# Float32 weights, unsplit, for the 64-slot experts: pairs of 64-column products on the two halves of the array, and the 192-slot expert in turns with the last one

## Chip, cores and metric

The kernel runs on one core of a Trainium2 chip. The metric is the device time of one execution in microseconds (us); the state before is given as the median of three runs and one profiled execution.

## What is computed

Two transformer blocks run over one sequence of 256 positions by 1024 features in float32. The first block has two layers (a mixer, then a feed-forward part); the feed-forward part of its second layer is a mixture of 8 SwiGLU experts, each position using the two that its router scores highest. The second block follows. The change touches the mixture of experts alone. Cut from the reference:

```python
def swiglu(x, w1, w3, w2):
    return (jax.nn.silu(x @ w1) * (x @ w3)) @ w2

def moe_swiglu(x, router_w, w1, w3, w2):            # t: 256 x 1024
    logits = (t @ router_w).astype(jnp.float32)
    top_v, top_i = lax.top_k(logits, TOP_K)         # 2 of 8
    gates = jax.nn.softmax(top_v, axis=-1)
    combine = jnp.sum(jax.nn.one_hot(top_i, N_EXPERTS, dtype=jnp.float32) * gates[..., None], axis=1)
    out = jnp.zeros_like(t)
    for e in range(N_EXPERTS):                      # w1[e], w3[e]: 1024 x 3584, w2[e]: 3584 x 1024
        out = out + combine[:, e:e + 1].astype(t.dtype) * swiglu(t, w1[e], w3[e], w2[e])
```

## The kernel before

**Slots.** After routing, experts 1 to 7 are ranked by how many positions chose them. Expert 0 and ranks 2 and 3 get 128 slots each, rank 1 gets 192 (128 and 64 more), ranks 4 to 7 get 64 each; if the positions don't fit, a second pass (`tc.If`) runs, which did not happen here. A one-hot matrix `oh` of positions by slots gathers the positions of an expert (`gather`, products of line 1169) and spreads the results back (`scatter`, line 1218).

**Steps.** An expert's 3584 hidden features go in 7 chunks of 512. One chunk of one expert is a step: it needs three tiles of 128 partitions x 4096 float32 (2 MB each): w1 and w3 for the up-products, w2 for the down-products. So there are 56 steps and 168 loads (`load`, line 155, all on SP's queue). They go through six buffers, `raw`, three in each of two pools, which the program takes in turn: a load waits until the load six before it has been read out. The down-products of a step stand behind the up-products of the next step.

**Groups.** Steps come in five groups: expert 0 in turns with rank 4, rank 2 with rank 5, rank 1 alone (its 128 and its 64 slots use each weight twice), rank 3 with rank 6, rank 7 alone. The tiles of the gathered positions are named g609, g876, g1167, g1365 and g1658 in the trace.

**Products.** Every weight is split into two float32r parts by `split`: ScalarE casts the high part, `wH` (line 170), VectorE subtracts to get the low part, `wL` (line 172). One split covers 128 x 1024; a step has 12 (4 for each of three tiles), and there are four buffers of each part. A 128-slot step forms three products for each tile of weights, `mm3`: high by high, low by high, high by low (lines 176 to 178). A 64-slot step puts the high and the low part of its 64 positions side by side as 128 stationary columns and forms two products, `mm2` (lines 1234 and 1235); the two halves of the result, copied out of PSUM (lines 1316 and 1317), are added by a product with a constant (`fold`, line 1336), before the activation (1339, 1340) and another split into `hO`. All moving operands here are 128 x 512. A 128-slot step transposes its hidden features four times (line 182) and splits them into `hH` and `hL`.

**Order.** The source says which instruction uses what; the order on each engine is made by the framework's planner when the kernel is built, from its own estimate of times. So transposes and folds stand among the up- and down-products. SP's loads stand in source order: w1, w3 of a step, then w2 of the step before.

**Elsewhere.** The mixers and the second block have float32 products that aren't split: line 943 (attention scores) takes its 64 contraction rows by turns from the lower and the upper half of the partitions, and 256 moving columns; line 747 has 64 x 64 products whose operands lie in one half of the partitions and whose results go by turns to PSUM partitions 0 to 63 and 64 to 127; lines 492 and 1548 use the whole array.

Of the kernel before, what the change touches and what calls it, by code (L numbers as in the profile page):

```python
# [105 lines left out]
class K:  # L106
# [1035 lines left out]
    def gather(self, xnH, xnL, pl, parts, into=None):  # L1142

        V, A, T = self.V, self.A, self.T
        if into is None:
            self.n += 1
            into = [self.mp.tile([P, 2, S], F32R, tag="oh", name=f"oh{self.n}", bufs=2), *self.xT_tiles(f"g{self.n}")]
        oh, gH, gL = into  # L1150
        for t in range(2):
            for over, r, slot0 in parts:
                for o in ((P, P + 64) if over else (0,)):
                    last = V.tensor_scalar(oh[:, t, o:o + (64 if over else P)], self.c("iota")[:, 0:64 if over else P],
                                           float(slot0), pl[:, t, r:r + 1], op0=OP.add, op1=OP.is_equal)
        if parts[0] == (False, 0, 0):
            self.hold = [(self.V, last)] * HOLD0

        c0 = P if parts[0][0] else 0
        w = P * (not parts[0][0]) + 64 * parts[-1][0]  # L1160
        m = 4 if w <= P else 2
        for k in range(0, KT, m):
            ks = slice(k, k + m)
            for src, low in ((xnH, False), (xnL, True)):
                b = self.bank()
                v = b.rearrange("p (k s) -> p k s", k=m)[:, :, 0:w]
# [4 lines left out]
                if not low:  # L1171
                    A.copy(gH[:, ks, c0:c0 + w], v)
                else:
                    if c0 == 0:
                        V.tensor_copy(gL[:, ks, 0:P], v[:, :, 0:P])
                    if c0 + w > P:
                        V.tensor_copy(gH[:, ks, P + 64:S], v[:, :, w - 64:w])
        return into

    def scatter(self, oh, cmp_, slots, accs, xacc, scale=1.0):  # L1180
# [5 lines left out]
        ohT, gcs, ys = [], [], []  # L1186
        for r, sl in slots:
            self.n += 1
            b = self.bank()
# [4 lines left out]
            o = self.mp.tile([P, S], F32R, tag="ohT", name=f"ohT{self.n}", bufs=2)  # L1194
            V.tensor_copy(o, b[:, 0:S])
            ohT.append(o)
# [3 lines left out]
            gcs.append(gc)  # L1200
        yield
        for i, (gc, acc) in enumerate(zip(gcs, accs())):

            h = tile(D, "rscr" if i else "yH")
            h = [h[:, ns] for ns in half]
            l = [self.wk(512, "ff", 3).bitcast(F32R) for n in half] if i else [tile(D, "yL")]
            l = l if i else [l[0][:, ns] for ns in half]
            for n in range(2):
                A.activation(h[n], acc[n], AF.Copy, scale=gc[:, 0:1])
                V.scalar_tensor_tensor(l[n], acc[n], gc[:, 0:1], h[n].bitcast(F32), op0=OP.mult, op1=OP.subtract)  # L1210
            ys.append((h, l))
        yield
        for t in range(2):
            for n in range(2):
                b = self.bank()
                for i in range(len(slots)):
                    for j, y in enumerate(ys[i]):
                        T.matmul(b, lhsT=ohT[i][:, t * P:(t + 1) * P], rhs=y[n], start=i == 0 and j == 0,
                                 stop=i == len(slots) - 1 and j == 1)
                V.scalar_tensor_tensor(xacc[:, t, half[n]], xacc[:, t, half[n]], scale, b, op0=OP.mult, op1=OP.add)  # L1220

    def experts(self, groups, xnH, xnL, pl, cmp_, xacc, between=None):
# [7 lines left out]
        main, over = slice(0, P), slice(P, 2 * P)  # L1230
# [6 lines left out]
        def down(job, c, hs, rd):  # L1237
            rd = rd.rearrange("p (f d) -> p f d", d=D)
            if c == 0:
                for o in hs:  # L1240
                    state["acc"][o] = [self.bank("acc") for n in range(2)]
            for j in range(4):
                H, L = self.split(rd[:, j:j + 1], (1, D))
                for n in range(2):
                    ns = slice(n * 512, n * 512 + 512)
                    ends = (c == 0 and j == 0, c == 6 and j == 3)
                    for o, h in hs.items():
                        acc = state["acc"][o][n]
                        if o:
                            mm2(acc, h[:, j], H[:, 0, ns], L[:, 0, ns], *ends)  # L1250
                        else:
                            self.mm3(acc, h[0][:, j], h[1][:, j], H[:, 0, ns], L[:, 0, ns], *ends)
# [3 lines left out]
        first = {id(g): (g[2][0], g[2][-1]) for g in groups}  # L1256
        pend, rest, into = None, None, None

        def gather(g, only=None):
            nonlocal into  # L1260
            parts = sorted(p for w, ps in g[0] for p in ps) if only is None else only
            into = self.gather(xnH, xnL, pl, parts, into if only and only[0][0] else None)

        late = None
        for n, (g, j, c) in enumerate(steps):
            w, parts = g[0][j]
            if between and g is groups[1]:
                between()
                between = None
            if (j, c) == first[id(g)][0]:  # L1270
                if len(g) > 3:

                    gather(g, g[3])
                    late = [p for p in sorted(p for w_, ps in g[0] for p in ps) if p not in g[3]]
                elif n == 0:
                    gather(g)
                oh, gH, gL = into
            if late and late[0] in parts:
                gather(g, late)
                late = None  # L1280
            raws = [self.load(w(c, i)) for i in range(2)]
            put = None
            if pend:
                (g0, j0, c0), hs = pend
                rd = self.load(g0[0][j0][0](c0, 2))
                if (j0, c0) == first[id(g0)][1]:
                    slots = [(r, over if o else main) for o, r, s in sorted(p for w_, ps in g0[0] for p in ps)]
                    put = self.scatter(state["oh"], cmp_, slots, lambda: [state["acc"][o] for o in sorted(state["acc"])],
                                       xacc, g0[1])
                    next(put)  # L1290
            banks, others = [], []
            kinds = [o for o, r, s in parts]
            for i in range(2):
                if False in kinds:
                    banks.append(self.bank())
                if True in kinds:
                    others.append(self.bank())
                x = raws[i].rearrange("p (k f) -> p k f", k=KT)
                for k in range(KT):
                    if k % 2 == 0:  # L1300
                        H, L = self.split(x[:, k:k + 2], (2, 512))
                    ends = (k == 0, k == KT - 1)
                    if banks:
                        self.mm3(banks[i], gH[:, k, main], gL[:, k, main], H[:, k % 2], L[:, k % 2], *ends)
                    if others:
                        mm2(others[i], gH[:, k, over], H[:, k % 2], L[:, k % 2], *ends)
# [3 lines left out]
            if banks:  # L1310
                s = self.wk(512, "ff", 3)
                A.activation(s, banks[0], AF.Silu)
                V.tensor_tensor(s, s, banks[1], OP.mult)
            if others:
                so = [self.wk(512, "ff", 3) for i in range(2)]
                A.copy(so[0], others[0])
                V.tensor_copy(so[1], others[1])  # L1317
            if n + 1 < len(steps) and steps[n + 1][0] is not g and len(steps[n + 1][0]) < 4:
                gather(steps[n + 1][0])
            if pend:  # L1320
                down(j0, c0, hs, rd)
            hs = {}
            self.n += 1
            if banks:
# [6 lines left out]
                hs[False] = (hH, hL)  # L1331
            if others:
                b = self.bank()
                for i in range(2):
                    for f in range(4):
                        T.matmul(b[:, i * 256 + f * 64:i * 256 + f * 64 + 64], lhsT=so[i][:, f * P:(f + 1) * P],  # L1336
                                 rhs=self.c("fold"), start=True, stop=True)
                s = self.wk(512, "ff", 3)[:, 0:256]
                A.activation(s, b[:, 0:256], AF.Silu)
                V.tensor_tensor(s, s, b[:, 256:512], OP.mult)  # L1340
                hO = self.mp.tile([P, 4, P], F32R, tag="hO", name=f"hO{self.n}", bufs=1)
                self.split(s.rearrange("p (f s) -> p f s", f=4), None, hO[:, :, 0:64], hO[:, :, 64:P])
                hs[True] = hO
# [3 lines left out]
            if (j, c) == first[id(g)][0]:  # L1347
# [4 lines left out]
        slots = [(r, over if o else main) for o, r, s in sorted(p for w_, ps in g0[0] for p in ps)]  # L1352
        put = self.scatter(state["oh"], cmp_, slots, lambda: [state["acc"][o] for o in sorted(state["acc"])], xacc, g0[1])
        down(j0, c0, hs, rd)
        list(put)

    def moe(self, xn):
# [21 lines left out]
        def pair(n, o, scale, order=None, now=None):  # L1379

            order = order or [(j, c) for c in range(7) for j in range(2)]
# [419 lines left out]
```

## Time and profile before

| | |
|---|---|
| median of 3 runs | 2092.45 us (2091.4 to 2101.74) |
| profiled execution | 2096.6 us, its span 2094.8 us |
| TensorE products (PE) | 1910.6 us busy, 91% of the span |
| VectorE (DVE) | 1613.3 us, 77% |
| ScalarE (ACT) | 1194.7 us, 57% |
| DMA | 484.79 MB, mean 231 GB/s over the span |
| mean granted TensorE clock | 0.944 of full speed |

PE is TensorE's row of products and PEld its row of weight loads; an engine's busy share is a mean over stages with different limits. The profile's page also cuts the span into 40 equal slices and gives for each the busy tenths of every engine and of the DMA engines, and the GB/s moved.

### The profile page before, as it was taken

How to read it: one execution, taken by the hardware profiler on the slowest of the kernel's cores; microseconds unless marked ns; L12 is line 12 of the kernel's file. 1: busy time of each engine (PE TensorE's matmuls, PEld its weight loads, DVE VectorE, ACT ScalarE, POOL GpSimd, SP SyncE). 2: the span in 40 equal slices, each digit the busy share in tenths (PEclk: the TensorE clock that was granted, in tenths of full speed). 3: DMA queues.
4: the chain of work that ended last, by engine and by line, in shares of the span. 5: the costliest groups of instructions: out<-in, count | busy, mean ns of one | idle time of the engine just before them, and what ended most of it. 6: DMA issues, size and time to landing. Idle time of an engine off the chain costs nothing. (4 is left out here: it accounts for less than half of the span.)

```text
span 2094.8 us, 28337 instructions
## 1 busy us (share of the span) xinstructions
PE 1910.6 (91%) x11072; PEld 1573.6 (75%) x11072; DVE 1613.3 (77%) x2131; ACT 1194.7 (57%) x1539; POOL 201.6 (10%) x128
## 2 busy tenths in 40 slices
PE   7878999977789999999999999999999886899998
PEld 6767899976577876776767888877677565779997
DVE  7895644579848998898888655699889887757776
ACT  3333444432335887777777554578777764645554
POOL 4241100043421000000000000000000003210000
PEclk9788999997788999999999999999999997889999
DMA  5321353542117999989998655589999953225451
GB/s 230 122 81 53 150 214 148 183 157 108 51 58 278 356 400 373 359 342 370 361 368 319 241 202 205 202 324 408 377 364 342 358 222 138 81 91 201 143 220 61
DMA packets 37581, 484.79 MB, mean 231 GB/s; under 512 B 4544, under 2 KB 5184, under 8 KB 8000
## 3 DMA queue, kind: packets, MB, share of 16 engines
q1 hardware_dynamic: 34992, 475.74, 59.8%
q10 hardware_dynamic: 2448, 7.17, 1.0%
q8 instruction: 89, 1.46, 0.3%
q14 instruction: 52, 0.43, 0.1%
HBM read 481.84 MB, written 1.05 MB: 231 GB/s over the span
## 5 line engine op out<-in xcount | busy, mean ns | idle before, releaser
L172 DVE TENSOR_TENSOR wL<-raw,wH 128x1024 fp32r<-128x1024 f32 x846 | 1001.3, 1223 | 257.4 <-ACT wH L170 253.2
L170 ACT CAST wH<-raw 128x1024 fp32r<-128x1024 f32 x896 | 917.3, 1049 | 489.6 <-PE mm L177 151.3
L177 PE MATMUL acc<-wL,hH 128*128 128x512 f32 x408 | 163.7, 402 | 0.2 <-DVE wL L172 0.2
L178 PE MATMUL acc<-wH,hL 128*128 128x512 f32 x408 | 160.8, 395 | 0.0
L176 PE MATMUL acc<-wH,hH 128*128 128x512 f32 x408 | 157.0, 398 | 0.7 <-ACT hH L170 0.7
L172 POOL TENSOR_TENSOR wL<-raw,wH 128x1024 fp32r<-128x1024 f32 x50 | 124.3, 2496 | 140.4 <-ACT wH L170 123.4
L188 POOL TENSOR_TENSOR sm_brs<-sm_brs,half_neg 128x1 f32<-128x1 f32 x8 | 12.1, 1517 | 1298.6 <-DVE sm_brs L186 1298.6
L176 PE MATMUL mm<-b2yH,wH 128*128 128x256 f32 x384 | 109.2, 285 | 0.0
L177 PE MATMUL mm<-b2yL,wH 128*128 128x256 f32 x384 | 109.1, 284 | 0.0
L178 PE MATMUL mm<-b2yH,wL 128*128 128x256 f32 x384 | 108.9, 284 | 0.0
L1235 PE MATMUL acc<-wL,hO 128*128 128x512 f32 x280 | 104.9, 418 | 0.8
L1234 PE MATMUL acc<-wH,hO 128*128 128x512 f32 x280 | 99.2, 398 | 1.4 <-DVE hO L172 1.4
L176 PE MATMUL mm<-y0H,wH 128*128 128x256 f32 x352 | 100.2, 285 | 0.0
L177 PE MATMUL mm<-y0L,wH 128*128 128x256 f32 x352 | 99.9, 284 | 0.0
L178 PE MATMUL mm<-y0H,wL 128*128 128x256 f32 x352 | 99.8, 284 | 0.0
L1336 PEld LDWEIGHTS mm<-cst,ff 128*128 128x128 f32 x560 | 75.2, 191 | 29.5 <-DVE ff L1317 19.5
L177 PEld LDWEIGHTS acc<-wL,hH 128*128 128x128 f32 x408 | 76.8, 188 | 17.4 <-DVE wL L172 1.1
L178 PEld LDWEIGHTS acc<-wH,hL 128*128 128x128 f32 x408 | 76.7, 188 | 17.4
L176 PEld LDWEIGHTS acc<-wH,hH 128*128 128x128 f32 x408 | 75.9, 188 | 17.8 <-ACT hH L170 1.4
L1336 PE MATMUL mm<-cst,ff 128*128 128x64 f32 x560 | 75.4, 269 | 13.8 <-DVE ff L1317 12.5
L176 PEld LDWEIGHTS mm<-b2yH,wH 128*128 128x128 f32 x384 | 74.1, 193 | 0.7 <-ACT b2yH L204 0.2
L177 PEld LDWEIGHTS mm<-b2yL,wH 128*128 128x128 f32 x384 | 74.1, 193 | 0.7 <-DVE b2yL L205 0.3
(569 smaller groups left out, 4294.4 us busy)
## 6 DMA issues: line engine op xcount, KB each, us to landing
raw<-in_moe_dram SPq DMA_DIRECT2D x168, 2048.0 KB, 9.6
raw<-in_ffn_dram SPq DMA_DIRECT2D x33, 2048.0 KB, 7.7
raw<-in_w_in_dram SPq DMA_DIRECT2D x13, 2048.0 KB, 8.1
raw<-in_w_o_dram SPq DMA_DIRECT2D x4, 2048.0 KB, 7.7
row<-in_ln_dram ACTq DMA_DIRECT2D x8, 512.0 KB, 3.7
raw<-in_w_out_dram SPq DMA_DIRECT2D x2, 2048.0 KB, 8.3
raw<-in_w_in_dram SPq DMA_DIRECT2D x3, 1024.0 KB, 4.9
raw<-in_ffn_dram SPq DMA_DIRECT2D x3, 1024.0 KB, 5.0
```

Of the source, the lines that this page charges most:

```text
L170: self.A.copy(H, src)
L172: (eng or self.V).tensor_tensor(L, src, H.bitcast(F32), OP.subtract)
L176: self.T.matmul(out, lhsT=lh, rhs=rh, start=start, stop=False)
L177: self.T.matmul(out, lhsT=lh, rhs=rl, start=False, stop=False)
L178: return self.T.matmul(out, lhsT=ll, rhs=rh, start=False, stop=stop)
L188: return self.G.tensor_tensor(out, out, self.half_neg.to_broadcast([P, n]), OP.pow)
L1234: T.matmul(out, lhsT=lh, rhs=rh, start=start, stop=False)
L1235: T.matmul(out, lhsT=lh, rhs=rl, start=False, stop=stop)
L1336: T.matmul(b[:, i * 256 + f * 64:i * 256 + f * 64 + 64], lhsT=so[i][:, f * P:(f + 1) * P], rhs=self.c("fold"), start=True, stop=True)
```

## The change

The 64-slot steps no longer use float32r parts. Their positions are gathered into one float32 tile `gx` (the low part is added to the copied high part), and the loaded weights go into the product as they are, float32, by `side`: two products for each tile of weights, each with the 64 positions as 64 stationary columns and one half of the weights' columns as the moving operand, the first writing PSUM partitions 0 to 63, the second 64 to 127. So a result of 64 x 512 lies in one PSUM tile of 128 x 256, and the activation, its product and two transposes work on 128 x 256. Splits, the two copies and the folds of these steps are gone; in the down-products the same is done with 1024 columns in two halves of 512, and one PSUM bank holds what two held. `scatter` reads the halves back by partition rows.

Rank 1 and rank 7 now form one group, in turns; the rank-1 steps use both forms (its 128 slots by `mm3`, its other 64 by `side`). So there are four groups, and their order is 0 and 4, 2 and 5, 1 and 7, 3 and 6.

```diff
     gather:
+            x = self.xp.tile([P, KT, 2, 64], F32, tag="xTL", name=f"gx{self.n}", bufs=1)
...
+                for i, r, slot0 in parts:
+                    u = v[:, :, at[i] - c0:at[i] - c0 + (64 if i else P)]
+                    d = i and gx[:, ks, i - 1]
+                    if i == 0:
+                        V.tensor_copy(gL[:, ks], u) if low else A.copy(gH[:, ks], u)
+                    elif low:
+                        V.tensor_tensor(d, d, u, OP.add)
+                    else:
+                        A.copy(d, u)
     experts:
-        def mm2(out, lh, rh, rl, start, stop):
-            T.matmul(out, lhsT=lh, rhs=rh, start=start, stop=False)
-            T.matmul(out, lhsT=lh, rhs=rl, start=False, stop=stop)
+        def side(out, lhsT, rhs, start, stop):
+            n = rhs.shape[1] // 2
+            for i in range(2):
+                T.matmul(out[i * 64:i * 64 + 64], lhsT=lhsT, rhs=rhs[:, i * n:i * n + n], start=start, stop=stop)
...
+            for i, h in hs.items():
+                acc = state["acc"][i]
+                for j in range(4):
+                    if i:
+                        side(acc[0], h[:, j % 2, (j // 2) * 64:(j // 2) * 64 + 64], rd[:, j], *ends)
+                    else:
+                        H, L = self.split(rd[:, j:j + 1], (1, D))
+                        for n in range(2):
+                            self.mm3(acc[n], h[0][:, j], h[1][:, j], H[:, 0, ns], L[:, 0, ns], *ends)
...
-                    if others:
-                        mm2(others[i], gH[:, k, over], H[:, k % 2], L[:, k % 2], *ends)
+                for p, b in nar:
+                    for k in range(KT):
+                        side(b[:, i * 256:i * 256 + 256], gx[:, k, p - 1], x[:, k], k == 0, k == KT - 1)
...
-                A.copy(so[0], others[0])
-                V.tensor_copy(so[1], others[1])
+            for p, b in nar:
+                sn.append(self.wk(512, "ff", 3)[:, 0:256])
+                A.activation(sn[-1], b[:, 0:256], AF.Silu)
+                V.tensor_tensor(sn[-1], sn[-1], b[:, 256:512], OP.mult)
...
-                        T.matmul(b[:, i * 256 + f * 64:i * 256 + f * 64 + 64], lhsT=so[i][:, f * P:(f + 1) * P],
-                                 rhs=self.c("fold"), start=True, stop=True)
...
+                    self.transpose(b[:, i * P:(i + 1) * P], s[:, i * P:(i + 1) * P])
+                h = self.mp.tile([P, 2, P], F32, tag="hN", name=f"hN{self.n}", bufs=1)
+                A.copy(h, b[:, 0:256].rearrange("p (f s) -> p f s", f=2))
     moe:
-                      ([(part(1), [(False, 1, 0), (True, 1, P)])], 1.0, chunks(0)),
-                      pair((3, 0), (6, 0), 1.0), ([(part(7), [(True, 7, 0)])], 1.0, chunks(0))], xnH, xnL, pl, cmp_, xn,
+                      ([(part(1), [(0, 1, 0), (1, 1, P)]), (part(7), [(2, 7, 0)])], 1.0, turns), (pair(3, 6), 1.0, turns)],
```

## Rows read from the trace of the kernel before

**Rows 1.** The page: busy us of each engine, then slices (busy tenths, GB/s).

```profile
PE 1910.6 (91%) x11072; PEld 1573.6 (75%) x11072; DVE 1613.3 (77%) x2131; ACT 1194.7 (57%) x1539; POOL 201.6 (10%) x128
...
DMA  5321353542117999989998655589999953225451
GB/s 230 122 81 53 150 214 148 183 157 108 51 58 278 356 400 373 359 342 370 361 368 319 241 202 205 202 324 408 377 364 342 358 222 138 81 91 201 143 220 61
```

**Rows 2.** Windows, the five groups: us, busy (x) by engine, PEclk, DMA share, GB/s.

```profile
657.00:892.00 235.00, 224.45 (x1034) 175.23 (x1034) 211.70 (x227) 183.03 (x206) 0.00 (x0) 0.99 0.96 371
892.00:1140.00 248.00, 234.41 (x1044) 176.66 (x1043) 222.16 (x235) 189.13 (x212) 0.00 (x0) 1.00 0.94 360
1140.00:1351.00 211.00, 210.39 (x1007) 175.20 (x1007) 128.35 (x147) 107.37 (x127) 0.00 (x0) 1.00 0.57 210
1351.00:1592.00 241.00, 233.05 (x1061) 181.19 (x1060) 217.54 (x222) 186.80 (x208) 0.00 (x0) 1.00 0.93 360
1592.00:1730.00 138.00, 120.14 (x502) 84.51 (x500) 119.12 (x132) 95.69 (x114) 0.00 (x0) 0.95 0.78 296
```

**Rows 3.** Groups by form, 892 to 1140: xcount | busy us, mean ns | idle before.

```profile
L172 DVE TENSOR_TENSOR wL<-raw,wH 128x1024 fp32r<-128x1024 f32 x170 | 197.2, 1218 | 4.7 <-ACT wH L170 4.5
...
L170 ACT CAST wH<-raw 128x1024 fp32r<-128x1024 f32 x168 | 171.5, 1050 | 25.9 <-PE mm L178 12.7 <-PE mm L1234 8.4 <-PE acc L178 2.9
...
L182 PE MATMUL mm<-cst,ff 128*128 128x128 f32 x28 | 4.2, 272 | 0.0
...
L1218 PE MATMUL mm<-yH,ohT 128*128 128x512 f32 x4 | 1.6, 393 | 0.0
```

**Rows 4.** Waits of SP's queue, 892 to 1140: us in total, times, longest.

```profile
SPq L155 <- DVE wL L172: 181.1, 35, 7.0
SPq L155 <- DVE ff L1340: 43.9, 7, 6.5
```

**Rows 5.** Timeline of PE in a 128-slot step: start us, us.

```profile
804.03 0.39 PE L176 MATMUL mm<-wH,g609H 128*128 128x512 f32 x1
804.26 0.40 PE L177 MATMUL mm<-wL,g609H 128*128 128x512 f32 x1
804.50 0.39 PE L178 MATMUL mm<-wH,g609L 128*128 128x512 f32 x1
804.73 0.39 PE L176 MATMUL mm<-wH,g609H 128*128 128x512 f32 x1
```

**Rows 6.** Lines with float32 operands: ns min/median/max; the first from the page.

```profile
L1336 PE MATMUL mm<-cst,ff 128*128 128x64 f32 x560 | 75.4, 269 | 13.8 <-DVE ff L1317 12.5
...
L1548 PE MATMUL acc<-xc,lw x32: 377/379/767, 1764.5 to 1789.5; 128*128 128x256 f32 x32
...
L492 PE MATMUL acc<-s,cst x16: 592/595/1219, 36.4 to 538.4; 128*128 128x512 f32 x16
```

**Rows 7.** Timeline of PE, three places with float32 products.

```profile
1764.54 0.59 PE L1548 MATMUL acc<-xc,lw 128*128 128x256 f32 x2
...
141.06 0.39 PE L178 MATMUL mm<-wH,x0L 128*128 128x512 f32 x1
141.38 1.13 PE L943 MATMUL mm<-aT,aT 64*128 64x256 f32 x8
...
151.41 0.65 PE L747 MATMUL acc<-s,cq 64*64 64x64 f32 x14
```

**Rows 8.** Windows in which the DMA engines were full; columns as in rows 2.

```profile
1410.00:1480.00 70.00, 67.95 (x309) 53.08 (x310) 66.23 (x64) 58.59 (x65) 0.00 (x0) 1.00 0.99 405
1430.00:1440.00 10.00, 10.00 (x47) 7.82 (x46) 9.60 (x10) 9.14 (x11) 0.00 (x0) 1.00 1.00 421
...
1620.00:1640.00 20.00, 18.46 (x78) 12.42 (x79) 18.30 (x19) 16.62 (x19) 0.00 (x0) 1.00 0.99 376
```

**Rows 9.** The last group: its up-products (line 1234), and a window.

```profile
L1234 PE MATMUL mm<-wH,g1658H x112: 387/394/628, 1592.7 to 1713.2; 128*128 128x512 f32 x112
...
1680.00:1700.00 20.00, 17.02 (x66) 12.68 (x65) 15.54 (x16) 13.04 (x15) 0.00 (x0) 0.83 0.90 349
```

More of the change, by code (lines that the diff above doesn't have):

```diff
@@ L1148, in gather @@
             self.n += 1
-            into = [self.mp.tile([P, 2, S], F32R, tag="oh", name=f"oh{self.n}", bufs=2), *self.xT_tiles(f"g{self.n}")]
-        oh, gH, gL = into
-        for t in range(2):
[L1152 to L1156, printed above, removed]
+            g = self.xp.tile([P, KT, S], F32R, tag="xTH", name=f"g{self.n}", bufs=1)
+            x = self.xp.tile([P, KT, 2, 64], F32, tag="xTL", name=f"gx{self.n}", bufs=1)
+            into = self.mp.tile([P, 2, 3 * P], F32R, tag="oh", name=f"oh{self.n}", bufs=2), g[:, :, 0:P], g[:, :, P:S], x
+        oh, gH, gL, gx = into
+        iota = self.c("iota")
+        for t in range(2):
+            for i, r, slot0 in parts:
+                for o, n in ((P, P),) if i == 0 else ((0, 64), (64, 64)) if i == 1 else ((2 * P, 64), (2 * P + 64, 64)):
+                    last = V.tensor_scalar(oh[:, t, o:o + n], iota[:, 0:n], float(slot0), pl[:, t, r:r + 1], op0=OP.add,
+                                           op1=OP.is_equal)
+        if parts[0] == (0, 0, 0):
             self.hold = [(self.V, last)] * HOLD0
-        c0 = P if parts[0][0] else 0
-        w = P * (not parts[0][0]) + 64 * parts[-1][0]
-        m = 4 if w <= P else 2
+        at = {0: P, 1: 64, 2: 2 * P}
+        c0 = min(at[i] for i, r, s in parts)
+        w = sum(64 if i else P for i, r, s in parts)
+        m = 512 // w if w != 192 else 2
         for k in range(0, KT, m):
@@ L1170, in gather @@
                                  start=t == 0, stop=t == 1)
[L1171 to L1177, printed above, removed]
+                for i, r, slot0 in parts:
+                    u = v[:, :, at[i] - c0:at[i] - c0 + (64 if i else P)]
[6 more added lines that the diff above has]
+                        A.copy(d, u)
         return into
@@ L1185, in scatter @@
         half = [slice(n * 512, n * 512 + 512) for n in range(2)]
-        ohT, gcs, ys = [], [], []
-        for r, sl in slots:
+        got = []
+        for i, r in slots:
             self.n += 1
+            sl = slice((P, 0, 2 * P)[i], (P, 0, 2 * P)[i] + P)
             b = self.bank()
@@ L1199, in scatter @@
             V.tensor_tensor(gc[:, 0:1], gc[:, 0:1], gc[:, 1:2], OP.add)
-            gcs.append(gc)
+            got.append((i, o, gc))
         yield
[L1202 to L1211, printed above, removed]
+        ys = []
+        for i, o, gc in got:
+            if i == 0:
+                h, l = tile(D, "yH"), tile(D, "yL")
+                h, l = ([x[:, ns] for ns in half] for x in (h, l))
+            elif i == 1:
+                h, l = ([x] for x in tile(D, "rscr").rearrange("p (a b) -> a p b", a=2))
+            else:
+                h, l = ([self.wk(512, "ff", 3).bitcast(F32R)] for n in half)
+            for n, acc in enumerate(accs()[i]):
+                A.activation(h[n], acc, AF.Copy, scale=gc[:, 0:1])
+                V.scalar_tensor_tensor(l[n], acc, gc[:, 0:1], h[n].bitcast(F32), op0=OP.mult, op1=OP.subtract)
+            ys.append((i, o, (h, l)))
         yield
@@ L1215, in scatter @@
                 b = self.bank()
[L1216 to L1219, printed above, removed]
+                ts = slice(t * P, (t + 1) * P)
+                rows = slice(n * 64, n * 64 + 64)
+                todo = [(o[:, ts], y[n]) if i == 0 else (o[rows, ts], y[0][rows]) for i, o, hl in ys for y in hl]
+                for j, (o, y) in enumerate(todo):
+                    T.matmul(b, lhsT=o, rhs=y, start=j == 0, stop=j == len(todo) - 1)
                 V.scalar_tensor_tensor(xacc[:, t, half[n]], xacc[:, t, half[n]], scale, b, op0=OP.mult, op1=OP.add)
@@ L1238, in down @@
+        def down(c, hs, rd):
             rd = rd.rearrange("p (f d) -> p f d", d=D)
             if c == 0:
[L1240 to L1245, printed above, removed]
-                    ends = (c == 0 and j == 0, c == 6 and j == 3)
[L1247 to L1252, printed above, removed]
@@ L1255, in experts @@
-        steps = [(g, j, c) for g in groups for j, c in g[2]]
[L1256 to L1264, printed above, removed]
+                for i in hs:
+                    state["acc"][i] = [self.bank("acc") for n in range(1 if i else 2)]
@@ new lines, in experts, with gather, put_of @@
+        steps = [(g, j, c) for g in groups for j, c in g[2]]
+        pend, rest, late, into = None, None, [], None
+        parts_of = lambda g: sorted(p for w, parts in g[0] for p in parts)
+        def gather(g):
+            nonlocal into, late
+            now = [p for p in parts_of(g) if len(g) < 4 or p in g[3]]
+            late = [p for p in parts_of(g) if p not in now]
+            into = self.gather(xnH, xnL, pl, now)
+        def put_of(g):
+            return self.scatter(state["oh"], cmp_, [p[0:2] for p in parts_of(g)], lambda: state["acc"], xacc, g[1])
@@ L1265, in experts @@
+        gather(groups[0])
         for n, (g, j, c) in enumerate(steps):
             w, parts = g[0][j]
+            new = n == 0 or steps[n - 1][0] is not g
             if between and g is groups[1]:
@@ L1269, in experts @@
                 between = None
[L1270 to L1277, printed above, removed]
+            if new:
+                oh, gH, gL, gx = into
             if late and late[0] in parts:
-                gather(g, late)
-                late = None
+                self.gather(xnH, xnL, pl, late, into)
+                late = []
             raws = [self.load(w(c, i)) for i in range(2)]
@@ L1285, in experts @@
                 rd = self.load(g0[0][j0][0](c0, 2))
[L1286 to L1289, printed above, removed]
+                if new:
+                    put = put_of(g0)
                     next(put)
-            banks, others = [], []
-            kinds = [o for o, r, s in parts]
+            main = [] if parts[0][0] else [self.bank() for i in range(2)]
+            nar = [(p, self.bank()) for p, r, s in parts if p]
             for i in range(2):
[L1294 to L1297, printed above, removed]
                 x = raws[i].rearrange("p (k f) -> p k f", k=KT)
-                for k in range(KT):
+                for k in range(KT if main else 0):
                     if k % 2 == 0:
                         H, L = self.split(x[:, k:k + 2], (2, 512))
-                    ends = (k == 0, k == KT - 1)
-                    if banks:
-                        self.mm3(banks[i], gH[:, k, main], gL[:, k, main], H[:, k % 2], L[:, k % 2], *ends)
-                    if others:
-                        mm2(others[i], gH[:, k, over], H[:, k % 2], L[:, k % 2], *ends)
+                    self.mm3(main[i], gH[:, k], gL[:, k], H[:, k % 2], L[:, k % 2], k == 0, k == KT - 1)
+                for p, b in nar:
+                    for k in range(KT):
+                        side(b[:, i * 256:i * 256 + 256], gx[:, k, p - 1], x[:, k], k == 0, k == KT - 1)
                 if i == 0 and rest:
@@ L1309, in experts @@
                     rest = None
-            if banks:
+            if main:
                 s = self.wk(512, "ff", 3)
[L1312 to L1315, printed above, removed]
-                A.copy(so[0], others[0])
-                V.tensor_copy(so[1], others[1])
-            if n + 1 < len(steps) and steps[n + 1][0] is not g and len(steps[n + 1][0]) < 4:
+                A.activation(s, main[0], AF.Silu)
+                V.tensor_tensor(s, s, main[1], OP.mult)
+            sn = []
+            for p, b in nar:
+                sn.append(self.wk(512, "ff", 3)[:, 0:256])
+                A.activation(sn[-1], b[:, 0:256], AF.Silu)
+                V.tensor_tensor(sn[-1], sn[-1], b[:, 256:512], OP.mult)
+            if n + 1 < len(steps) and steps[n + 1][0] is not g:
                 gather(steps[n + 1][0])
             if pend:
-                down(j0, c0, hs, rd)
+                down(c0, hs, rd)
             hs = {}
             self.n += 1
-            if banks:
+            if main:
                 b = self.bank()
@@ L1346, in experts @@
                 rest = put
-            if (j, c) == first[id(g)][0]:
+            if new:
                 state.update(acc={}, oh=oh)
@@ L1351, in experts @@
         rd = self.load(g0[0][j0][0](c0, 2))
-        slots = [(r, over if o else main) for o, r, s in sorted(p for w_, ps in g0[0] for p in ps)]
-        put = self.scatter(state["oh"], cmp_, slots, lambda: [state["acc"][o] for o in sorted(state["acc"])], xacc, g0[1])
-        down(j0, c0, hs, rd)
+        put = put_of(g0)
+        next(put)
+        down(c0, hs, rd)
         list(put)
@@ L1397, in moe @@
         with self.tc.If(most[0] > P):
-            self.experts([([(part(r), [(False, r, s)])], 1.0, chunks(0)) for r, s in (
+            self.experts([([(part(r), [(0, r, s)])], 1.0, alone) for r, s in (
                 (0, P), (1, WIDE), (2, P), (3, P), (4, 64), (5, 64), (6, 64), (7, 64))], xnH, xnL, pl, cmp_, xn)
```

35 lines of the change are left out of this document (13 added, 22 removed).

## The prediction, as it was put on record before the run

> **What bounds the kernel now.** I read the page first: PE is busy for 91% of the span, but the slices show where the others join it. In slices 13 to 22 the DMA engines are at eight to nine tenths and more, at 319 to 400 GB/s, and fall to five tenths for four slices [rows 1]. So I cut the experts by their tiles into the five groups [rows 2]. They last 1073 us of 2094.8, and they have three different limits.
>
> The three groups in turns take 235, 248 and 241 us for 14 steps each, 35 us for a pair of steps. In the second one DVE is busy 222 of 248 us, PE 234, DMA moves 360 GB/s [rows 2]. The groups by form say what DVE does: 170 low parts in 197.2 us, 1.16 us each, so 12 a step make 13.9 us and a pair 27.8 [rows 3]. ACT's casts wait for PE and SP's loads wait for the low parts: 181.1 us of SP's waits end with `wL`, another 43.9 with a vector instruction of the same steps [rows 4]. So DVE and PE hold each other up, and both hold the loads. The rank-1 group is bound by PE: 210.39 of 211 us, DVE at 128, DMA at 210 GB/s. The last group is the reverse: PE 120 of 138, the rest waiting for parts, hidden features and loads [rows 2].
>
> **The change, part by part.** *PE, a 128-slot step.* Its 72 products of 512 columns stay. Four starts lie 0.70 us apart for three intervals, 0.233 each [rows 5], so 16.8 us; four transposes at 4.2/28 = 0.15 us add 0.6 [rows 3]. Together 17.4.
>
> *PE, a 64-slot step.* Its 48 products of 512 columns (11.2 us) and the folds go. What comes is float32 on half the array, which no row shows in just this shape; I build it from two facts. First, the fold has 8 products in 35 steps, 280, and the trace has 560 records: a float32 product is two records. One lasts 377 ns for 256 columns and 592 for 512 [rows 6], so 215/256 = 0.84 ns a column, and two whole-array records of 256 columns begin 0.59 - 0.38 = 0.21 us apart [rows 7]. A product of 256 columns therefore takes 0.427 us, two of them 0.853 if they follow each other. Second, whether the halves run side by side. Eight records of line 943, in turns on the two halves of the rows, take 1.13 us, so (1.13 - 0.38)/7 = 0.107 us each, half of 0.21. For column halves line 747 is the nearest: 14 records of 64 columns in 0.65 us, (0.65 - 0.22)/13 = 0.033 each, where 64 x 0.84 = 0.053 would be one after the other [rows 7]. So the bounds for a pair of 256 columns are 0.427 (side by side) and 0.853 (in turn); I take 0.427, because both kinds of half show overlap. The weight loads of 64 columns are inside those 0.033 us. A step has 16 such pairs for up and 4 of twice the width for down, 24 units: 10.25 us, with two transposes 10.55. In turn it would be 20.8.
>
> *Switching.* Line 943 starts 0.32 us after the product before it, not 0.23 [rows 7], so going from the whole array to half costs 0.1; six switches in a pair of steps, 0.6 us. The Trainium skill says in "TensorEngine Tiling (Array Packing)", Key Properties, that changing the tiling mode drains TensorE; it speaks against this change, and if a switch cost a whole 0.39 us product, six would make 2.3. The row stands nearer to the small price, and the sum goes by the row.
>
> *A pair then.* PE: 17.4 + 10.55 + 0.6 = 28.6 us. DVE: 12 low parts instead of 24, 13.9 us and some 2 of small work; ACT likewise. Neither bounds any more. The loads of a 64-slot step now go free when PE has read them, not when DVE has: SP waits for PE. That is no delay by itself: at 5.27 us a load (below) a buffer may be held for four loads' time, 21 us, after it landed before the queue runs dry, and PE needs 3.4 us for each of w1 and w3. What can be late next is the split of the 128-slot w2: the first product needs a cast (1.05) and the second a low part (1.22) [rows 3], and where these stand behind the activation of the 64-slot step, PE idles up to 3 us a pair. From both sides: 0 and 3; I take 1.5, since ACT and DVE are half idle but queue in order. PE: 30.1.
>
> *DMA.* A pair loads 12.58 MB. At full DMA engines the windows show 405 GB/s over 70 us, 421 at best and 376 at worst [rows 8]: 31.1, 29.9 and 33.5 us. I take the middle of best and worst, 398: 31.6 us, or 5.27 a load. So a pair becomes DMA-bound, 31.6 against 35.
>
> *The groups.* 0 and 4: six loads are in before it starts, so PE sets 7 x 30.1 = 210. 2 and 5: 7 x 31.6 = 221. 3 and 6: 221. 1 and 7: PE does 17.4 + 2 x 10.55 + 0.9 = 39.4, with 1 us of stalls 40.4, times seven 283; in the pairs the gather and scatter at a border lie under DMA, here they are on PE, a scatter's 16 products (four rows like line 1218's 1.6) and a gather about as much, 7: 290. The end: 16.8 us from the last group's last up-product to 1730 [rows 2, 9]; the down-products no longer wait for splits there, but two sets of slots are scattered instead of one: 13. Gather's extra adds and copies, eight of each per group, lie on the freed ACT and DVE; on the path they would be 2 us a group.
>
> Sum: 210 + 221 + 290 + 221 + 13 = 955 against 1073, 118 us less. The profiled execution took 2096.6 us, 1.8 around its span and 0.2% above the median of 2092.45; 118 off it is 1978.6, and off the median **1974 us**.
>
> **The rivals.** *The halves run in turn (slower).* Place: every `side` pair. With 0.853 a 64-slot step costs 20.8, a pair 38.8, the rank-1 pair 59.9: 3 x 272 + 426 + 16 = 1258, 185 more: 2277. It decides at 15.5 us a step, 0.635 a unit: from there on the change is no gain. For it: line 747's operands span 64 partitions, here both moving streams come from all 128. Against it: [rows 7]. The change would not do what it says then; 1 in 10.
>
> *DMA gives no more than it gives now.* At 360 GB/s [rows 2] a pair takes 35.0: 215 + 245 + 300 + 245 + 17 = 1022, so 2041. For it: the DMA share is already 0.93 to 0.96 in those groups, and one full window has only 376. Against it: 405 for 70 us with the same kind of loads, while DVE was as busy as ever. The Trainium skill, "DMA: Bandwidth & Descriptors", Where 436 GB/s comes from, says that for HBM to SBUF the HBM side binds at about 358 GB/s per core; the 405 and 421 of this trace lie above that, so it can't be a ceiling for this core alone. 15 in 100.
>
> *PE waits for loads and loses its clock.* In the last group, where PE was 17.0 of 20 us busy with waits between, the granted clock was 0.83 for 20 us [rows 9], a mix of 1.2 and 2.4 GHz. At 0.83 the pair's PE work is 34.4 us: 3 x 241 + 290 + 14 = 1027, 2046. Against it: PE's share in a pair would be 28.6/31.6, higher than there, and a slower PE closes the gaps that slowed it. 8 in 100.
>
> **Chances and range.** My forecast has 67 in 100, its own range 1940 to 2010 (stalls 0 to 3, DMA 421 to 376). With the best DMA and no stalls it is 200 + 209 + 281 + 209 + 9 = 908, or 1927. The range goes from 1925 to 2050, taking in the slow DMA and the clock. The three runs spread over 0.5%, so 0.5% is about what a measurement tells from no change. Faster 0.88, within 0.5% 0.02 (a partly lost overlap near 0.635), slower 0.10.
>
> **What would show it.** In the changed kernel's trace: records of 128 x 256 and 128 x 512 on 128 rows and 64 columns, two for each product, two starts within some 0.22 us for 256 columns (right) or one (wrong); 336 fewer low parts of line 172's form; SP's loads waiting for PE rather than for `wL`; 390 GB/s or more through three groups and some 310 in the group of ranks 1 and 7; 31 to 32 us a pair, 39 to 41 in that group. It is wrong if a 64-slot step's PE time is far from 10.5, if GB/s stays near 360 with loads queued, or if the clock leaves 1.00 inside the groups.

## The result

The changed kernel takes 1997.78 us (median of 4 runs, 1994.05 to 2001.83), the kernel before 2092.05 on the same chip: ratio 0.9548, 95% interval 0.9509 to 0.9588, 94 us less. The forecast was 1974 in a range of 1925 to 2050, so the sign and the range held and the gain is 24 us smaller than forecast. The profiled execution took 2001.22 us, 95.4 less than the one before.

The page of the changed kernel (busy us of each engine; DMA busy tenths and GB/s in 40 slices; the lines of the new products, of the low parts, and of the silu of the 64-slot step):

```profile
PE 1819.5 (91%) x11670; PEld 1408.2 (70%) x11670; DVE 1197.6 (60%) x1717; ACT 842.3 (42%) x1176; POOL 203.4 (10%) x128
...
DMA  6320536352204799999999777787999944134551
GB/s 241 118 94 23 190 137 243 127 215 85 95 13 169 282 430 418 388 393 355 363 393 384 300 297 305 307 342 315 365 414 390 399 156 164 43 135 171 185 195 64
...
L172 DVE TENSOR_TENSOR wL<-raw,wH 128x1024 fp32r<-128x1024 f32 (+1 forms) x510 | 616.3, 1229 | 261.9 <-ACT wH L170 250.7
...
L1247 PE MATMUL mm<-raw,gx 128*64 128x256 f32 x2240 | 252.3, 381 | 0.0
...
L1247 PE MATMUL acc<-raw,hN 128*64 128x512 f32 x560 | 127.5, 597 | 0.0
L1321 ACT ACTIVATE ff<-mm 128x256 f32<-128x256 f32 x35 | 13.5, 385 | 247.8 <-PE mm L1247 247.8
```

VectorE is 416 us less busy than in [rows 1], ScalarE 352, PE only 91. The records are those that the prediction named: 35 x 64 and 35 x 16, two for a product. But one line was not expected: ScalarE stood idle for 247.8 us ahead of the 35 silu of line 1321.

The same windows as [rows 2], now four groups and the end (us, busy by engine, granted clock, DMA share, GB/s):

```profile
655.00:875.00 220.00, 208.33 (x1164) 147.00 (x1163) 117.23 (x133) 102.09 (x123) 0.00 (x0) 0.98 0.96 390
875.00:1112.00 237.00, 219.72 (x1165) 149.84 (x1163) 120.64 (x146) 100.86 (x126) 0.00 (x0) 0.96 0.95 374
1112.00:1399.00 287.00, 287.00 (x1744) 184.07 (x1743) 129.56 (x140) 108.05 (x139) 0.00 (x0) 1.00 0.79 309
1399.00:1614.00 215.00, 203.45 (x1105) 138.26 (x1104) 108.76 (x111) 91.86 (x106) 0.00 (x0) 0.98 0.97 388
1614.00:1632.00 18.00, 15.67 (x70) 8.75 (x66) 10.19 (x18) 6.61 (x9) 0.00 (x0) 1.00 0.02 7
```

They sum to 977 us against 1073: 96 less, the whole gain. Against the forecast: 220 for 210, 237 for 221, 287 for 290, 215 for 221, 18 for 13. The rank-1 group came out as worked out, with PE busy throughout. In the second group PE is busy for 93%, VectorE for half of the time; the DMA engines' share is 0.95, but they move only 374 GB/s, where slices of the same kernel show 430. What waits there is seen in the timeline of one pair of steps. ScalarE first (start us, us; in brackets the idle time before it and what ended that):

```profile
936.01 0.39 ACT L1321 ACTIVATE ff<-mm 128x256 f32<-128x256 f32 x1 [6.48 <-PE mm L1247]
937.37 0.37 ACT L1342 COPY hN<-mm 128x256 f32<-128x256 f32 x1 [0.98 <-PE mm L182]
...
953.41 0.59 ACT L1316 ACTIVATE ff<-mm 128x512 f32<-128x512 f32 x1
962.06 0.59 ACT L170 CAST hH<-mm 128x512 fp32r<-128x512 f32 x1 [8.06 <-PE mm L182]
969.13 0.39 ACT L1321 ACTIVATE ff<-mm 128x256 f32<-128x256 f32 x1 [6.48 <-PE mm L1247]
970.49 0.37 ACT L1342 COPY hN<-mm 128x256 f32<-128x256 f32 x1 [0.98 <-PE mm L182]
970.76 3.89 ACT L170 CAST wH<-raw 128x1024 fp32r<-128x1024 f32 x4
```

And PE in the same stretch:

```profile
961.95 7.13 PE L1247 MATMUL mm<-raw,gx 128*64 128x256 f32 x64
970.02 0.44 PE L182 MATMUL mm<-cst,ff 128*128 128x128 f32 x2 [0.94 <-DVE ff L1322]
971.86 1.22 PE L176 MATMUL acc<-wH,hH 128*128 128x512 f32 x2 [1.41 <-ACT wH L170]
973.12 0.80 PE L177 MATMUL acc<-wL,hH 128*128 128x512 f32 x1
```

A pair lasts 33.12 us here (936.01 to 969.13). At 962.65 ScalarE is done with the hidden features and idles for 6.48 us, until the up-products of the 64-slot step are finished; only behind silu and copy come the four casts of w2 of the 128-slot step, whose down-products PE is to do next. So PE waits 0.94 us for the silu's product and 1.41 for the first cast, and in this pair the granted clock falls right after: 0.57 over the 8 us from 971 to 979, where the down-products are. Summed over the group, PE's waits by cause are 8.5, 5.6 and 2.3 us, 16.4 in six pairs:

```profile
PE acc L176 <- ACT wH L170: 8.5, 6, 1.5
PE mm L182 <- DVE ff L1322: 5.6, 6, 0.9
PE acc L177 <- DVE wL L172: 2.3, 5, 0.5
```

### The profile page after: what moved, and what is told of

It reads as the page before. It is cut to its first block, busy times and chain, and to the rows that moved or that the text cites. A ratio compares the mean times of both kernels' runs of the same rounds, so it can differ in the third digit from the quotient of the medians.

```text
span 1999.4 us, 28155 instructions
## 1 busy us (share of the span) xinstructions
PE 1819.5 (91%) x11670; PEld 1408.2 (70%) x11670; DVE 1197.6 (60%) x1717; ACT 842.3 (42%) x1176; POOL 203.4 (10%) x128
## 5 line engine op out<-in xcount | busy, mean ns | idle before, releaser
L172 DVE TENSOR_TENSOR wL<-raw,wH 128x1024 fp32r<-128x1024 f32 (+1 forms) x510 | 616.3, 1229 | 261.9 <-ACT wH L170 250.7
L170 ACT CAST wH<-raw 128x1024 fp32r<-128x1024 f32 x560 | 577.5, 1051 | 401.7 <-PE mm L177 154.0
L1247 PE MATMUL mm<-raw,gx 128*64 128x256 f32 x2240 | 252.3, 381 | 0.0
L1247 PEld LDWEIGHTS mm<-raw,gx 128*64 128x64 f32 x2240 | 156.6, 137 | 85.6 <-issue 10.8
L176 PE MATMUL acc<-wH,hH 128*128 128x512 f32 x408 | 163.8, 416 | 19.8 <-ACT wH L170 19.0
L176 PE MATMUL mm<-wH,g 128*128 128x512 f32 x448 | 177.1, 395 | 0.0
L177 PE MATMUL mm<-wL,g 128*128 128x512 f32 x448 | 175.1, 391 | 0.0
L178 PE MATMUL mm<-wH,g 128*128 128x512 f32 x448 | 174.8, 390 | 0.0
L1247 PE MATMUL acc<-raw,hN 128*64 128x512 f32 x560 | 127.5, 597 | 0.0
L1321 ACT ACTIVATE ff<-mm 128x256 f32<-128x256 f32 x35 | 13.5, 385 | 247.8 <-PE mm L1247 247.8
L1322 DVE TENSOR_TENSOR ff<-ff,mm 128x256 f32<-128x256 f32 x35 | 14.7, 421 | 157.2 <-ACT ff L1321 157.2
```

Of the source, the lines that this page charges most:

```text
L170: self.A.copy(H, src)
L172: (eng or self.V).tensor_tensor(L, src, H.bitcast(F32), OP.subtract)
L176: self.T.matmul(out, lhsT=lh, rhs=rh, start=start, stop=False)
L177: self.T.matmul(out, lhsT=lh, rhs=rl, start=False, stop=False)
L178: return self.T.matmul(out, lhsT=ll, rhs=rh, start=False, stop=stop)
L1247: T.matmul(out[i * 64:i * 64 + 64], lhsT=lhsT, rhs=rhs[:, i * n:i * n + n], start=start, stop=stop)
```

## The experiments

**Theory A**: ScalarE's order sets the pair: w2's casts stand behind the silu of the 64-slot step, PE idles, and the clock that it loses makes the next products slower still; DMA is not the bound. **Rival B**, the forecast's own: a pair is bound by its six loads. **Rival C**: the halves overlap only in part. The changed kernel was run again on the chip of experiments 1 to 3; experiments 4 to 6 ran on another (before: 2085.53), so ratios are compared there.

> The changed kernel once more, as the base for the others of this call: 1994 to 2002 us, a pair of steps in the group of ranks 2 and 5 at 33 us, in the first two pairs of the last group 28.2.

1993.25 us, ratio 0.9528 (0.9495 to 0.9562).

**1. w2's casts ahead of the silu.** The down-products of the waiting 128-slot step are issued ahead of the 64-slot step's activation, and the silu is held behind their last cast:

```diff
-        self.A.copy(H, src)
+        self.cast = self.A.copy(H, src)
...
+            if pend and not main:
+                down(c0, hs, rd)
...
-                A.activation(sn[-1], b[:, 0:256], AF.Silu)
+                with self.tc.issue_after(self.cast.ins) if pend and not main else nullcontext():
+                    A.activation(sn[-1], b[:, 0:256], AF.Silu)
...
-            if pend:
+            if pend and main:
                 down(c0, hs, rd)
```

> In steps of 64 slots alone, the casts of the waiting 128-slot w2 are put ahead of the activation on ScalarE, nothing else. Theory A (ScalarE's order is what costs a pair 33 us where 28.2 is possible: w2 lies in its buffer 10 us and more while ScalarE waits for the 64-slot up-products): some 14 pairs lose 4 to 5 us each, 1928 to 1945 us, granted clock 1.00 through the groups, a pair at 28.2 to 29.5. Theory B (the loads set the pace, and the order only hides it): pairs stay at 31 or more, 1975 to 1995 us. If theory A holds the loads show 425 to 433 GB/s as the next limit.

1942.86 us (1940.78 to 1944.23), ratio 0.9269 (0.925 to 0.9289): 50 us less than the changed kernel, 153 less than the one before. ScalarE and PE in a pair of this kernel:

```profile
942.14 0.59 ACT L170 CAST hH<-mm 128x512 fp32r<-128x512 f32 x1 [8.07 <-PE mm L182]
942.62 3.89 ACT L170 CAST wH<-raw 128x1024 fp32r<-128x1024 f32 x4
949.20 0.39 ACT L1324 ACTIVATE ff<-mm 128x256 f32<-128x256 f32 x1 [2.70 <-PE mm L1247]
...
970.30 0.59 ACT L170 CAST hH<-mm 128x512 fp32r<-128x512 f32 x1 [8.07 <-PE mm L182]
```

```profile
942.03 7.13 PE L1247 MATMUL mm<-raw,gx 128*64 128x256 f32 x64
949.09 0.73 PE L176 MATMUL acc<-wH,hH 128*128 128x512 f32 x2
949.65 0.40 PE L177 MATMUL acc<-wL,hH 128*128 128x512 f32 x1
...
954.81 0.38 PE L182 MATMUL mm<-cst,ff 128*128 128x128 f32 x2
```

The four casts now run beside the 64 records, the down-products follow them without a gap, and a pair is 28.16 us (942.14 to 970.30). The edit moved more than ScalarE's casts: on PE, too, the 24 down-products now stand ahead of the two transposes of the 64-slot step (954.81), which before stood first and waited for the silu's product. No run parts the two orders. The windows of the five stretches, and of four pairs:

```profile
655.00:863.00 208.00, 204.14 (x1166) 145.80 (x1165) 117.47 (x137) 101.34 (x124) 0.00 (x0) 0.99 0.97 403
863.00:1077.00 214.00, 212.50 (x1174) 147.06 (x1175) 123.53 (x149) 101.92 (x129) 0.00 (x0) 0.99 1.00 422
1077.00:1362.00 285.00, 285.00 (x1732) 182.36 (x1731) 127.10 (x138) 106.14 (x137) 0.00 (x0) 1.00 0.80 317
1362.00:1562.00 200.00, 200.00 (x1113) 137.53 (x1113) 114.46 (x117) 95.57 (x111) 0.00 (x0) 1.00 0.97 403
1562.00:1577.00 15.00, 13.66 (x62) 7.89 (x61) 5.78 (x13) 2.33 (x4) 0.00 (x0) 0.99 0.47 196
...
926.00:1039.00 113.00, 113.00 (x635) 78.78 (x634) 64.92 (x61) 56.12 (x65) 0.00 (x0) 1.00 1.01 430
```

922 us in all, 55 less than after the change, 53 of them in the three groups that take 128 and 64 slots in turns and at the end. PE is busy for all of the last row at full clock, with DMA at 430 GB/s: the bytes are the same as in the changed kernel, so its 374 were no ceiling. A holds, for the order on ScalarE and PE together; B is refuted.

**2. One half after the other.** All products of a step's up-chain for one half of the array, then all for the other; the same products and bytes:

```diff
-        def side(out, lhsT, rhs, start, stop):
+        def side(out, lhsT, rhs, start, stop, half=None):
...
-            for i in range(2):
+            for i in range(2) if half is None else [half]:
...
-                    for k in range(KT):
-                        side(b[:, i * 256:i * 256 + 256], gx[:, k, p - 1], x[:, k], k == 0, k == KT - 1)
+                    for e in range(2):
+                        for k in range(KT):
+                            side(b[:, i * 256:i * 256 + 256], gx[:, k, p - 1], x[:, k], k == 0, k == KT - 1, e)
```

> Up-products of the 64-slot steps: all 8 products of one half of the array, then all 8 of the other, instead of pairs; down-products unchanged; same work and result. If the gain needs the pairs side by side (two halves at once only when neighbours in the order): up takes 13.7 us instead of 6.9 a step, 6 to 7 us more in 21 pairs and 13.7 in 7, 2180 to 2240 us, slower than before. If the halves overlap whatever the order: 1994 to 2002. If they never overlapped at all: no change either, but then the records would lie 0.21 us apart in both.

2174.06 us, ratio 1.0364 (1.0332 to 1.0395): slower than before the change, a little under the 2180 to 2240 expected. PE of this kernel, in the same place of a pair, then two windows inside the 64 records (980 to 981, 981.5 to 983):

```profile
978.90 11.61 PE L1247 MATMUL mm<-raw,gx 128*64 128x256 f32 x64
991.44 0.44 PE L182 MATMUL mm<-cst,ff 128*128 128x128 f32 x2 [0.93 <-DVE ff L1323]
993.29 0.73 PE L176 MATMUL acc<-wH,hH 128*128 128x512 f32 x2 [1.41 <-ACT wH L170]
...
979.82 1.46 PE L1247 MATMUL mm<-raw,gx 128*64 128x256 f32 x6
...
981.33 1.95 PE L1247 MATMUL mm<-raw,gx 128*64 128x256 f32 x12
```

64 records take 11.61 us instead of 7.13. From the first start to the last, a record is (7.13 - 0.38)/63 = 0.107 us in the changed kernel, (11.61 - 0.38)/63 = 0.178 here; the records' own length is 0.38 in both. But 0.178 is a mean of two paces. Inside a run on one half a record begins (1.46 - 0.38)/5 = 0.216 us after the one before, no sooner than on the whole array (0.21, [rows 7]). Only around the three places where the chain goes over to the other half does it come down: (1.95 - 0.38)/11 = 0.143 over the twelve records of the second window. So records on the same half do not overlap at all, and those on opposite halves do when they stand close to each other in the queue. C falls: the halves run side by side in the changed kernel, and here the up-products run in turn but for those places, as in the forecast's first rival.

**3. The old five groups** with float32 halves (rank 1 and rank 7 each alone):

```diff
-                      ([(part(1), [(0, 1, 0), (1, 1, P)]), (part(7), [(2, 7, 0)])], 1.0, turns), (pair(3, 6), 1.0, turns)],
+                      ([(part(1), [(0, 1, 0), (1, 1, P)])], 1.0, alone), (pair(3, 6), 1.0, turns),
+                      ([(part(7), [(2, 7, 0)])], 1.0, alone)],
```

> Float32 halves kept, but the five groups of before: rank 1 alone, then 3 and 6, then rank 7 alone. If the regrouping matters as the load times say: rank 1 alone 7 x 29 + 7 = 210, rank 7 alone at the pace of its loads 7 x 15 = 105 and the end, against 286 together: 25 to 45 us slower than the changed kernel, 2020 to 2040. If float32 alone makes the gain: within 10 us of 1998.

2015.02 us, ratio 0.961 (0.956 to 0.966), some 20 us more than the changed kernel on that chip, under the 25 to 45 expected and over the 10 of the other answer; these runs lie 22 us apart (2003.95 to 2025.51), so the 20 is rough. Most of the gain is the float32 halves, and the new grouping brings about a fifth of it. Rank 7 alone takes 88 us (1548 to 1636), not the 105 that its loads were expected to need.

**4. Fillers in the gaps.** To part the idle time from the clock:

```diff
...
+                if pend and not main and p == 1:
+                    self.warm(4, up)
                 b = self.bank()
                 for i in range(2):
                     self.transpose(b[:, i * P:(i + 1) * P], s[:, i * P:(i + 1) * P])
+                if pend and not main and p == 1:
+                    self.warm(6, self.tlast)
```

> The changed kernel, its two gaps on PE in a pair filled with products of zeros that nothing reads: four ahead of the transposes of the 64-slot step, six ahead of the down-products of the waiting 128-slot step (0.85 and 1.28 us, where the gaps are 0.94 and 1.41). ScalarE's order stays. Theory A (the idle itself costs 2.35 us a pair, and the granted clock that falls to half after it another 2.0 to 2.5): the clock stays at 1.00, the 24 down-products take 5.6 to 5.8 us instead of 6.3 to 8.6, a pair 31 instead of 33, and 13 such pairs give 26 to 30 us: 1960 to 1972. Rival (the down-products are slow because casts and low parts arrive late, the clock is a bystander): the down-products stay at 7.8, 1985 to 2000.

2002.19 us, ratio 0.9594 (0.9573 to 0.9615): a miss for A's total, and for its price of the clock; by the ratio it is no faster than the changed kernel (0.9528). Windows of four pairs and of the down-products in one, the changed kernel first (with one more pair of it, 778.2 to 809.8), then the one with fillers:

```profile
914.00:1046.00 132.00, 121.49 (x631) 82.86 (x630) 64.06 (x60) 55.75 (x64) 0.00 (x0) 0.94 0.96 378
971.00:979.00 8.00, 7.10 (x17) 5.20 (x18) 5.89 (x6) 5.74 (x6) 0.00 (x0) 0.57 0.99 420
...
778.20:809.80 31.60, 28.73 (x160) 19.58 (x162) 15.87 (x15) 13.96 (x17) 0.00 (x0) 1.00 1.00 411
```

```profile
918.00:1044.00 126.00, 123.84 (x673) 84.73 (x672) 61.74 (x60) 54.39 (x64) 0.00 (x0) 1.00 0.98 393
974.00:982.00 8.00, 7.46 (x32) 5.41 (x31) 7.05 (x7) 7.12 (x8) 0.00 (x0) 1.00 1.00 426
...
973.32 1.64 PE L309 MATMUL mm<-zero 128*128 128x512 f32 x6
974.98 0.73 PE L176 MATMUL acc<-wH,hH 128*128 128x512 f32 x2
976.24 0.50 PE L177 MATMUL acc<-wL,hH 128*128 128x512 f32 x1 [0.53 <-DVE wL L172]
```

The clock stays at 1.00 (2.4 GHz), where it was a mix of 1.2 and 2.4, and the pair shown falls from 33.1 to 31.6 us: the lost clock is worth 1.5 us of it, where I had expected 2.0 to 2.5. The down-products still take 6.5 us (974.98 to 981.50), since the first low part comes 1.26 us after the first product, not 0.56 as in experiment 1. The changed kernel itself says the same. Counted from one cast of `hH` to the next it has twelve stalled pairs, 31.6 to 33.9 us and 32.5 in the mean. In eight the granted clock is below 1.00; in the other four, with idle times of the same length, it stays at 1.00, and they last 31.6 us (778.2 to 809.8 is one), as those with fillers do. So over the twelve the clock is worth 0.9 us, and the gaps with what comes late behind them 3.4. What the clock gives back is used up elsewhere: where the casts had stood early (28.2 us, the first pairs of the first group and of the last) the ten fillers are on the path and make 30.5, and at the borders they cost some 2 us each.

**5. One load in three left out.** w3 is not loaded, the products for w3 read w1: the hidden features are not the reference's, PE's and ScalarE's work is the same. Once in the kernel of experiment 1, once in the changed kernel, where the scheduler then puts w2's casts ahead of the silu by itself.

```diff
-            raws = [self.load(w(c, i)) for i in range(2)]
+            raws = [self.load(w(c, 0))] * 2
```

> The kernel with w2's casts first, its w3 not loaded: the up-products of both halves read w1, so the hidden features are not the reference's; PE, ScalarE and VectorE have the same work, DMA has two loads a step instead of three. Theory A (PE sets a pair, 28.16 us, loads only look tight): pairs stay at 28.1 to 28.2, 1930 to 1945, some microseconds won at borders at most. Rival (loads at 4.84 us each, 29.0 a pair, now set the pace through their queue): 20 us or more faster, under 1922.

> The changed kernel, its w3 not loaded (hidden features not the reference's, as above). Nothing is pinned, but the scheduler, which prices fewer loads, now puts w2's casts ahead of the silu of the 64-slot step in ScalarE's queue by itself. Theory A (only that order matters, not bytes): as the kernel with w2's casts first, pairs of 28.1 to 28.3, 1930 to 1950. Rival (the 33 us pairs come from loads as well): the two kernels with two loads a step differ, or both lie 20 us or more under the kernel with w2's casts first.

1930.73 us, ratio 0.9253 (0.922 to 0.9286), and 1932.5 us, ratio 0.9274 (0.9253 to 0.9296): both intervals overlap that of experiment 1. Four pairs of the changed kernel without w3:

```profile
892.00:1005.00 113.00, 113.00 (x637) 78.72 (x635) 65.61 (x61) 56.98 (x65) 0.00 (x0) 1.00 0.80 310
```

Again 28.2 us a pair, with a third of the bytes gone. With the order right, the loads cost nothing that can be measured. And the order is not in the kernel's text: the same text gave the changed kernel pairs of 33 and of 28 us, and with one load in three left out 28 throughout, since the planner then puts the casts early. That its own estimate of the loads' time decides this is likely, but no run shows it.

**6. Old groups with w2's casts first**, both edits together.

> w2's casts first, float32 halves, but the five old groups (rank 1 and rank 7 each alone). Theory A (regrouping saves one border, a gather and a scatter with nothing beside them; loads are ahead of PE either way): rank 1 takes 29 us a step, rank 7 11.9, together about what their common group takes, and 8 to 20 us more than with the new groups: 1950 to 1963. Rival (rank 7 alone is held by its loads, 3 x 4.84 = 14.5 us a step): 18 us more on top, 1968 to 1985.

1958.59 us, ratio 0.9378 (0.9349 to 0.9406). Against 0.9269 that is 1.1% of 2090, 23 us: a little over A's 8 to 20 (its range of 1950 to 1963 held), short of its rival's 26 or more. The last expert alone takes 90 us for seven steps at 429 GB/s:

```profile
1485.00:1575.00 90.00, 83.23 (x594) 46.44 (x596) 12.42 (x24) 8.53 (x19) 0.00 (x0) 1.00 1.01 429
```

That is under the 103 us that 21 loads last at this rate (21 x 2.097 MB / 429 GB/s), since its first loads had landed before. PE's waits from 1485 to 1592 are mostly for the product of the silu, once in each step, and hardly for loads:

```profile
PE mm L182 <- DVE ff L1325: 6.6, 7, 0.9
PE mm L1247 <- DMA raw<-in_moe_dram: 1.0, 1, 1.0
PE acc L1247 <- DMA raw<-in_moe_dram: 0.8, 1, 0.8
```

So a 64-slot step that has no 128-slot step beside it leaves PE idle there, and the grouping saves this and a border. How the 23 us divide between the two is not shown.

## Why the prediction was right, and where it was off

**The halves run side by side: right.** 0.427 us was taken for a pair of float32 products; four records at 0.107 make 0.428. Experiment 2 shows the other bound: four records at 0.216 make 0.86, where the forecast had 0.853 for products in turn. Since its down-products still go in pairs and the runs overlap where they meet, a 64-slot step's products take 11.61 + 3.65 = 15.3 us there, near the 15.5 from which the forecast saw no gain; with the stall on top, that kernel is slower than before.

**PE's 28.6 us a pair: right.** Without stalls it is 28.16, so the switches cost no more than the 0.6 that was taken (the pair of experiment 1 has four of them, not six). The Trainium skill's rule of a drain ("TensorEngine Tiling (Array Packing)", Key Properties) would have given some 30.3 by the forecast's price of it; the row does not agree with that much.

**The stall behind the activation: the right place, a third of its size.** "PE idles up to 3 us a pair ... I take 1.5". Measured in the pair shown: 33.12 - 28.16 = 5.0 us, of them 2.35 of idle time, 0.7 for the first low part, 1.5 for the clock, some 0.4 left over; in the mean of the stalled pairs 32.5 - 28.2 = 4.3. The idle time alone, 16.4 us in six pairs, was inside the forecast's bound of 3 a pair; what had been priced only as a separate rival, the loss of the clock, follows the waits in most pairs and belonged in the same term. Twelve pairs at 4.3 are 52 us; experiment 1 gave back 50. The Trainium skill, "Perfetto Trace Analysis", Tensor Engine Instruction, says that ScalarE and VectorE take their queues strictly first in, first out; this trace agrees: ScalarE idles 6.48 us with casts behind the silu.

**"So a pair becomes DMA-bound", 31.6 us: this step failed.** The number is near the 33 that came, but by luck: the reason is another. With the order mended DMA gives 430 GB/s for 113 us, where the forecast took 398 from the middle of [rows 8]; its windows lay in a kernel whose loads waited for buffers. The Trainium skill, "HBM Reference", Specifications (TRN2), gives about 425 GB/s for a core that streams alone; the trace agrees, a little above it. Six loads at 430 are 29.3 us, a little more than PE's 28.16, so DMA falls slowly behind within a group, on loads that had landed early; the group of ranks 1 and 7, at 317 GB/s, lets it catch up.

**Groups and end.** Groups one and two came 10 and 16 us above the forecast (in both the stall: group one had been given 1.5 a pair for it, group two the pace of its loads), the group of ranks 1 and 7 and the last one 3 and 6 below. The end took 18 us, not 13: its 24 down-products of the waiting 128-slot step (1617.1 to 1623.8) stand on the path, and there too they wait for casts. Sum +22, and the median came out 24 above. Two errors that partly cancelled, DMA too slow and PE's stall too small, kept the total near.

**Its own signs.** VectorE forms exactly the 336 low parts fewer (842 to 506 of the 128x1024 form), and a pair in the group of ranks 1 and 7 takes 39.4 us, as said. But only one of the three other groups reached 390 GB/s (390, 374, 388), SP's loads wait not only for PE (510.7 us) but still 335.7 us for `wL`, and the clock left 1.00 inside the groups, which the forecast had named as a sign of being wrong.

## What to carry to other kernels

When an edit frees an engine, look at the order of its queue and not only at its busy share: ScalarE was 42% busy and still set the pace, because a wait for the 64-slot products stood ahead of work that was ready. Price an idle gap on PE together with the clock that it can cost, and read the DMA ceiling from a stretch whose loads do not wait for buffers. Alternate the halves product by product: here a run of eight products on one half, then eight on the other, lost the whole gain.

## What had not been expected of the hardware

Two halves of the columns, each with all 128 rows streaming, ran float32 records of 256 columns at 0.107 us each when they alternated; in a run on one half they began 0.216 us apart, as on the whole array (0.21). Gaps of 0.94 and 1.41 us on PE, in a stretch otherwise full, were followed by a granted clock of 0.57 over 8 us (a mix of 1.2 and 2.4 GHz) in one pair; after gaps of the same length it fell in some pairs and stayed at 1.00 in others, and the runs do not show what decides. With the gaps filled by products of zeros it stayed at 1.00 through the groups (661 to 1632 us). One core took 430 GB/s over 113 us with PE busy throughout.
